# Hybrid encoder layer on one core: the first stage's hand-written order, with places for other work behind every dense product instead of every third, and two product pairs of a scan step placed apart

## The chip, the core and the metric

The program runs on one core of a Trainium2 chip. A core has engines that work side by side: TensorE (PE; weight loads into it are shown as PEld), VectorE (DVE), ScalarE (ACT) and GpSimd (POOL); SyncE (SP) issues most DMAs. Each engine takes its instructions strictly in the order in which they were written into its queue, and waits on semaphores for the others. The metric is the device time of one execution in microseconds (us), lower being better.

## The reference

One layer of an encoder over 16 learned tokens and 1024 positions of width 1024, in float32. A normed input is projected into the inputs of two mixers and two gates; the first mixer is a gated DeltaNet with 8 heads, scanned forwards and backwards:

```python
h = rmsnorm(h_res, norm1_w[l])
proj = h @ w_in[l]
(q, k, v, z, b_raw, a_raw, sc_b, sc_c, sc_x, gate_a, gate_b) = jnp.split(proj, SPLIT_POINTS, axis=-1)
o_dn = gated_deltanet_bidir(q, k, v, z, b_raw, a_raw, dn_conv_w[l], A_log[l], dt_bias[l], dn_norm_w[l])
y_a = o_dn @ w_branch_dn[l]
y_b = (sc_b * depthwise_conv_centred(sc_c * sc_x, sc_conv_w[l])) @ w_branch_sc[l]
merged = jax.nn.sigmoid(gate_a) * y_a + jax.nn.sigmoid(gate_b) * y_b
h_res = h_res + merged @ w_out[l]
...
h_res = h_res + (jax.nn.silu(gu[..., :D_FF]) * gu[..., D_FF:]) @ w_down[l]
```

One chunk of the scan, for each head and direction, carries a state S (128 x 128):

```python
v_new = u_c - jnp.einsum("bhcd,bhde->bhce", w_c, S)
o_c = (jnp.einsum("bhcd,bhde->bhce", qd_c, S)
       + jnp.einsum("bhij,bhje->bhie", qk_c, v_new))
S = S * gl_c[..., None, None] + jnp.einsum("bhcd,bhce->bhde", kd_c, v_new)
```

## The kernel before

**Stages.** The first stage, to about 1061 us, computes all projections of the normed input but the last three z units, and all of the DeltaNet heads; the branches, the output projection and the gated MLP follow. The change lies in the first stage alone.

**Two kinds of work on TensorE.** The dense work is 69 units of 128 output columns each: 24 for q, k, v (three per head), 24 of the short convolution, 16 gates, 5 z. A unit is two or three banks, that is output tiles of 320 to 512 columns in PSUM (the memory in which products accumulate, in banks of 512 float32 columns per partition); a bank takes 24 products (8 pieces of the inner dimension, times high x high, high x low and low x high parts). `dense_steps` (L332) issues them, all from L339. Between them go the *streams*, Python generators that each carry one head through one phase: `g_decay`, `g_norm`, `g_inv` (inverses of the triangular blocks, put together from 32 x 32 pieces) and `g_scan` (the scan). VectorE's long element-wise jobs (convolutions, the substitution of `fs_job`, norms) wait as filler in three lanes.

**The order is written out by hand.** While the program is generated, the clocks `T["pe"]`, `T["dve"]`, `T["act"]` and `T["pool"]` keep planned times; here this bookkeeping is called the planner. `pe(ns)` moves TensorE's clock on and returns it plus HOP (200 ns); `V(n)` and `A(n)` price a VectorE or ScalarE operation of n columns, start it no earlier than TensorE's clock, and return its end plus TOPE (370 ns). A stream issues some instructions and yields the planned time from which its next ones may be issued. Each time a dense unit yields, the main loop (L1328) calls `run_streams` (L967), which resumes every stream whose time has come, and `pump` (L316), which issues filler to VectorE until its clock is 700 ns ahead of TensorE's. Where in each engine's queue an instruction stands is thus settled by the planner; what it waits for is settled by the data, through semaphores.

**Where a unit yields.** `dense_steps` yields behind every third product, having added the price of three. A product of n columns is priced n/2.4 + 13 ns. At four such places (`SPL`, L1323) the split of the next unit's weights into high and low parts is issued in four pieces (L942 and L945): a ScalarE cast, a VectorE subtraction, twice.

**One step of a scan** (L798 to L878) treats two chunks, one forwards (d = 0) and one backwards (d = 1), with two PSUM banks b1 and b2:

1. L805: kT by S into columns 0 and 1 of b1; L808: qT by S into columns 0 and 1 of b2.
2. L815, VectorE: r from b1 and the scaled values vS.
3. L820: NP (the inverse) by r into columns 2 and 3 of b1.
4. ScalarE, from these columns: w twice (L827), then v2 twice (L832; the profile calls it v).
5. L837, the *state products*: kn by w into columns 0 and 1 of b1. L840, the *decayed products*: PQ by v2 into columns 2 and 3 of b2.
6. L849, VectorE: the new S from b1; then the step's output from b2 (L867 to L877).

There are 8 heads of 8 steps; the last step of a head has no state products, so there are 56 pairs of L837 and 64 of L840. A matmul in float32 shows in the profile as two passes, so one pair is a group "x4". The two pairs of point 5 are issued at one place, when w is planned to be ready.

**Inverse and start of a scan.** In `g_inv` four groups of small products (L711, L720 with L723, L741 with L742, L748 with L749) are priced 600, 1050, 1000 and 1000 ns. In `g_scan` the first product (L787) may be issued 1000 ns before the planned time of the last vS (L779).

Of the kernel before, what the change touches and what calls it, by code (L numbers as in the profile page):

```python
# [16 lines left out]
P = 128  # L17
# [30 lines left out]
def encoder_layer(ctx: ExitStack, tc: tile.TileContext, x, meta, norm1_w, w_in, w_ba,  # L48
# [22 lines left out]
    def psm():  # L71
        return ps.tile([P, 512], F32, tag="m", name=uid("pm"), bufs=2)
# [187 lines left out]
    HOP, TOPE, DEP = 200, 370, 127  # L260
    ARRIVE = 10000
    LAND = 5500
    T = {"pe": 0.0, "dve": 0.0, "act": 0.0, "pool": 0.0}

    def on(e, ns, ready=0.0):

        T[e] = max(T[e], ready, T["pe"]) + ns
        return T[e] + TOPE

    def pe(ns):  # L270
        T["pe"] += ns
        return T["pe"] + HOP
# [4 lines left out]
    def A(n):  # L277
        return on("act", 144 + 0.834 * n)
# [49 lines left out]
                lanes[k].pop(0)  # L328

    sweep = ()  # L330

    def dense_steps(po, w, xx, t0, n):  # L332
        (wh, wl), (xh, xl) = w, xx
        t0 += C0
        parts = {"hh": (wh, lambda k: xh[:, k]), "hl": (wh, lambda k: xl[k]), "lh": (wl, lambda k: xh[:, k])}
        seq = [(m, k) for m in sweep for k in range(KT)] if sweep else [(m, k) for k in range(KT) for m in ("hh", "hl", "lh")]
        for i, (m, k) in enumerate(seq):
            ww, f = parts[m]
            mm(po[:, :n], ww[:, k], f(k)[:, t0:t0 + n], start=i == 0, stop=i == 3 * KT - 1)  # L339
            if i % 3 == 2:  # L340
                pe(3 * (n / 2.4 + 13))
                yield

    raws = []
# [6 lines left out]
    def half_buffer():  # L351
        return d1.tile([P, 520], F32, tag="rb", name=uid("rb"), bufs=3)
# [109 lines left out]
    def u_z(h, w):  # L462

        rest = None
        for i in range(2):
            po = psm()
            for k, _ in enumerate(dense_steps(po, w, hx, META + 512 * i, 512)):
                if k == 3 and rest:
                    rest()
                yield  # L470
            th = half_buffer()[:, :512]
            nc.scalar.activation(th, po, AF.Tanh, scale=0.5)
            A(512)

            def rest(i=i, th=th, po=po):
                nc.vector.scalar_tensor_tensor(out=th, in0=th, scalar=1.0, in1=po, op0=ALU.add, op1=ALU.mult)
                V(512)
                nc.sync.dma_start(z_d[h][:, 512 * i:512 * i + 512], th)
        T["dve"] = max(T["dve"], T["act"] + HOP)
        rest()  # L480
# [143 lines left out]
    def g_inv(h, st_):  # L624
# [35 lines left out]
        for j in range(META - 1):  # L660
            n = META - 1 - j
            tm = dn.tile([1, 64], F32, tag="tmm", name=uid("tm"), bufs=1)
            tv = tm[:, :(j + 1) * n].rearrange("p (r i) -> p r i", r=j + 1)
# [45 lines left out]
        for c in range(NC):  # L709
            for d, a, b, Xs, xo in pairs:  # L710
                mm(pt[B(b), c], NP[B(a), c, d, B(b)], Xs[B(a), c, xo:xo + 32], start=True, stop=True)  # L711
        pe(600)
        yield T["pe"] + HOP
        nc.scalar.mul(T2, pt, -1.0)
        yield A(256)
# [2 lines left out]
        for c in range(NC):  # L718
            for d, a, b, Xs, xo in pairs:
                mm(pp[B(a), c], T2[B(b), c], NP[B(b), c, d, B(b)], start=True, stop=True)  # L720
            for d, a, b, Xs, xo in pairs:
                if Xs is X64:
                    mm(px[B(b), c], NP[B(b), c, d, B(b)], T2[B(b), c], start=True, stop=True)  # L723
        pe(1050)
        yield T["pe"] + HOP
        for i, (d, a, b, Xs, xo) in enumerate(pairs):
            if i % 2:
# [12 lines left out]
        for c in range(NC):  # L740
            mm(pt[hi, c], NP[lo, c, 0, hi], X64[lo, c], start=True, stop=True)  # L741
            mm(pt[lo, c], NP[hi, c, 1, lo], X64[hi, c], start=True, stop=True)  # L742
        yield pe(1000)
        nc.scalar.mul(T3, pt, -1.0)
        yield A(512)
        pp = pss().rearrange("p (c i) -> p c i", c=NC)
        for c in range(NC):
            mm(pp[lo, c], T3[hi, c], NP[hi, c, 0, hi], start=True, stop=True)  # L748
            mm(pp[hi, c], T3[lo, c], NP[lo, c, 1, lo], start=True, stop=True)  # L749
        yield pe(1000)  # L750
        nc.scalar.copy(NP[lo, :, 0, hi], pp[lo])
        nc.vector.tensor_copy(NP[hi, :, 1, lo], pp[hi])
        yield max(on("dve", 710), A(512))
# [2 lines left out]
    def g_scan(h, st_):  # L756
# [9 lines left out]
        def newbank():  # L766
            return pss().rearrange("p (a n) -> p a n", a=4)

        for grp in ((8, 0, 7), (1, 2, 3), (4, 5, 6)):
# [7 lines left out]
            for i, c in enumerate(grp):  # L777
                p = META if c == 8 else P
                nc.scalar.activation(vS[:p, c], pt[:p, i], AF.Copy, scale=sk[:p, c:c + 1])  # L779
                A(P)  # L780
        yield T["act"] + HOP - 1000

        oacc = [NP[:, c, c // 4] for c in range(NC)]

# [14 lines left out]
        for i in range(NC):  # L799
            cd = (i, NC - 1 - i)  # L800
            hd = (h, 8 + h)
            act_ = [d for d in range(2) if S[d] is not None]
            b1, b2 = newbank(), newbank()
            for d in act_:
                mm(b1[:, d], kT[:, cs(cd[d])], S[d], start=True, stop=True)  # L805
            t = pe(215 * len(act_))
            for d in act_:
                mm(b2[:, d], qT[:, cs(cd[d])], S[d], start=True, stop=True)  # L808
            pe(215 * len(act_))
            yield t  # L810
            r0 = [vS[:, cd[0]], vS[:, cd[1]]]
            for d in act_:
                c = cd[d]
                r0[d] = dn.tile([P, P], F32, tag=f"r{d}", name=uid("r0"))
                nc.vector.scalar_tensor_tensor(out=r0[d], in0=b1[:, d], scalar=negEG[:, c, hd[d]:hd[d] + 1], in1=vS[:, c],  # L815
                                               op0=ALU.mult, op1=ALU.add)
                t = V(P, 1)
            yield t
            for d in range(2):
                mm(b1[:, 2 + d], NP[:, cd[d], d], r0[d], start=True, stop=True)  # L820
            yield pe(430)
            w = [None, None]
            v2 = [None, None]
            for d in range(2):
                c = cd[d]
                w[d] = dn.tile([P, P], F32, tag=f"w{d}", name=uid("w"))
                nc.scalar.activation(w[d], b1[:, 2 + d], AF.Copy, scale=ce[:, c, d:d + 1])  # L827
                t = A(P)
            for d in range(2):
                c = cd[d]  # L830
                v2[d] = dn.tile([P, P], F32, tag=f"v2{d}", name=uid("v2"))
                nc.scalar.activation(v2[d], b1[:, 2 + d], AF.Copy, scale=cc[:, c, d:d + 1])  # L832
                A(P)
            yield t
            if i < NC - 1:
                for d in range(2):
                    mm(b1[:, d], kn[:, cd[d]], w[d], start=True, stop=True)  # L837
                t = pe(430)
            for d in range(2):
                mm(b2[:, 2 + d], PQ[:, cd[d], d], v2[d], start=True, stop=True)  # L840
            t2 = pe(430)
            if i < NC - 1:
                yield t
                for d in range(2):
                    Sn = dn.tile([P, P], F32, tag=f"S{d}", name=uid("S"), bufs=2)
                    if S[d] is None:
                        nc.vector.tensor_copy(Sn, b1[:, d])
                    else:
                        nc.vector.scalar_tensor_tensor(out=Sn, in0=S[d], scalar=eGl[:, cd[d], hd[d]:hd[d] + 1],  # L849
                                                       in1=b1[:, d], op0=ALU.mult, op1=ALU.add)  # L850
                    t = V(P, 1)
                    S[d] = Sn
            else:
                freed += 1
                yield t2

            for d in range(2):
                c = cd[d]
                eg = eG[:, c, hd[d]:hd[d] + 1]
                first = c not in seen  # L860
                seen.add(c)
                if d not in act_:
                    nc.scalar.copy(oacc[c], b2[:, 2 + d])
                    A(P)
                    continue
                if first:
                    nc.scalar.activation(oacc[c], b2[:, d], AF.Copy, scale=eg)  # L867
                    A(P)
                else:
                    nc.vector.scalar_tensor_tensor(out=oacc[c], in0=b2[:, d], scalar=eg, in1=oacc[c],  # L870
                                                   op0=ALU.mult, op1=ALU.add)
                    V(P, 1)
                nc.vector.tensor_tensor(out=oacc[c], in0=b2[:, 2 + d], in1=oacc[c], op=ALU.add)
                V(P)
                if not first:
                    jk = dn.tile([P, P], F32, tag="jk", name=uid("jk"))
                    nc.scalar.activation(jk, oacc[c], AF.Square, accum_out=sso[:, c:c + 1])  # L877
                    on("act", 310)  # L878
            yield t
# [440 lines left out]
                yield T["act"]  # L1320

    dn = ph1.enter_context(tc.tile_pool(name="dn", bufs=1))
    SPL = (11, 12, 13, 14)  # L1323
    for g in (gen0, gen1):
        for _ in g:
            pass
    decs.append([g_gates(), T["pe"], None])
    while done < H or qkv_units or fill_units or any(ahead):  # L1328
        u = ahead.pop(0)
        if u is None:  # L1330
            run_streams()
            pump()
            T["pe"] += 100
            ahead.append(pick())
            continue
        for k in range(u[3][0], 4):
            split_part(u, k)
        if ahead[0]:
            ahead[0][1] = wtiles([P, KT, P])
        ahead.append(pick())  # L1340
        for n_, _ in enumerate(u[0][1](u[1])):
            if ahead[0] and n_ in SPL:
                split_part(ahead[0], SPL.index(n_))
            run_streams()
            pump()
# [198 lines left out]
    t = KT - 1  # L1544
# [41 lines left out]
    for j in range(NF):  # L1586
# [9 lines left out]
        if j >= HK:  # L1596
            k = j - HK
# [176 lines left out]
```

## Time and profile before

| | |
|---|---|
| median of 3 runs | 2012.12 us (2009.04 to 2012.36) |
| the profiled execution's own time | 2009.61 us |
| its span, first to last instruction | 2007.9 us |
| granted TensorE clock in the span | 0.999 |
| last product of L339 begins | 1060.7 us |
| DVE busy, ACT busy in the span | 1353.8 us, 823.9 us |

How to read the lines that follow. The page gives busy time, its share of the span and the number of instructions of each engine; the row PEclk shows the granted clock in 40 slices of the span, in tenths. A line of stretches begins with the stretch in us and its length, then the busy time (and count) of PE, PEld, DVE, ACT and POOL, the granted clock, the DMA share and GB/s. A line of a group names line, engine, operation, tile names (out<-in) and count, then the shortest, median and longest duration in ns; under it stand the causes of the engine's idle time before such an instruction, with the total in us and the number of times, or those who waited for the group. A row of the timeline gives start, duration (both us), engine, line, operation, tiles, shape, the number of instructions merged in it, and in brackets the engine's idle time before it with what ended it. Matmuls overlap in the array, so a product's duration is longer than the distance to the next start; it is the starts that tell the pace.

### The profile page before, as it was taken

Reading aid. Unit: us, or ns where it says so; the run is one execution under the profiler, and the core shown is the slowest. Engines: PE = TensorE matmul, PEld = TensorE weight load, DVE = VectorE, ACT = ScalarE, POOL = GpSimd, SP = SyncE. Lnnn points to the kernel's source line nnn. Section 1 sums busy time; section 2 is a strip of 40 time slices with the busy share of each in tenths; the row PEclk is TensorE's granted clock in tenths of the full one; section 3 lists DMA queues with packets and bytes.
Section 4 is the critical chain, followed back from the end, with each engine's and each line's share of the span. In section 5 each row is a group of like instructions: output and inputs, shape, how many; then the busy total and the mean of one; then the engine's idle time right before and its main releaser. Section 6 shows DMA issues by size and latency. Waiting matters only on the chain.

```text
span 2007.9 us, 31943 instructions
## 1 busy us (share of the span) xinstructions
PE 1987.4 (99%) x12059; PEld 1727.9 (86%) x12059; DVE 1353.8 (67%) x2966; ACT 823.9 (41%) x1945; POOL 119.6 (6%) x407
## 2 busy tenths in 40 slices
PE   9999999999999999999999999999999999999998
PEld 8999999999999988988888888887888888888887
DVE  6889586888888776866245434468866666646575
ACT  6462345454554464633334211224423333334344
POOL 2002200101020202010000000000000000000000
PEclk9999999999999999999999999999999999999999
DMA  3121222212212232232127633123666345477654
GB/s 138 40 88 64 75 78 71 74 47 76 59 54 85 69 101 64 81 89 94 70 94 247 215 126 116 58 90 109 237 225 221 139 149 186 158 272 244 196 172 167
DMA packets 131409, 247.85 MB, mean 123 GB/s; under 512 B 45045, under 2 KB 54694, under 8 KB 128823
## 3 DMA queue, kind: packets, MB, share of 16 engines
q1 hardware_dynamic: 130679, 244.77, 36.1%
q8 instruction: 94, 1.54, 0.3%
q10 hardware_dynamic: 576, 1.05, 0.1%
q14 instruction: 60, 0.49, 0.1%
HBM read 179.10 MB, written 66.67 MB: 122 GB/s over the span
## 4 chain that ended last, share of the span: by engine, by line
PE 90%; DVE 5%; ACT 2%; DMA 1%; issue 1%; SPq 0%; ACTq 0%; DVEq 0%
PE pm L339 36%; PE pd L1514 10%; PE pe L1514 4%; PE pm L1514 3%; PE pe L589 1%; PE pd L820 1%; PE pe L134 1%; PE pe L135 1%; PE pe L133 1%; PE pd L840 1%; PE pd L134 1%; PE pd L133 1%; PE pd L135 1%; PE pe L1682 1%; PE pe L1680 1%; PE pd L837 1%
## 5 line engine op out<-in xcount | busy, mean ns | idle before, releaser
L339 PE MATMUL pm<-hTh,wh 128*128 128x512 f32 (+4 forms) x1424 | 518.2, 369 | 0.8 <-ACT kq L391 0.5
L339 PE MATMUL pm<-hTh,wl 128*128 128x512 f32 (+4 forms) x1424 | 483.4, 344 | 0.0
L339 PE MATMUL pm<-al,wh 128*128 128x512 f32 (+4 forms) x1424 | 482.6, 343 | 0.0
L339 PEld LDWEIGHTS pm<-hTh,wh 128*128 128x128 f32 x1424 | 267.0, 188 | 20.4 <-issue 1.7
L339 PEld LDWEIGHTS pm<-hTh,wl 128*128 128x128 f32 x1424 | 266.1, 188 | 19.8 <-DVE wl L942 0.3
L339 PEld LDWEIGHTS pm<-al,wh 128*128 128x128 f32 x1424 | 267.4, 189 | 14.5
L101 DVE TENSOR_TENSOR al<-raw,ring_h 128x1024 fp32r<-128x1024 f32 x73 | 88.8, 1224 | 65.4 <-ACT ring_h L100 64.6
L942 DVE TENSOR_TENSOR wl<-raw,wh 128x512 fp32r<-128x512 f32 x134 | 91.0, 690 | 51.0 <-ACT wh L945 50.5
L100 ACT CAST ring_h<-raw 128x1024 fp32r<-128x1024 f32 x73 | 76.8, 1055 | 106.8 <-PE pd L1682 35.5
L361 DVE SCALAR_TENSOR_TENSOR kq<-ra,wc,kq 128x520 f32<-128x520 f32 x128 | 96.9, 757 | 3.3 <-ACT kq L391 1.7
L945 ACT CAST wh<-raw 128x512 fp32r<-128x512 f32 x134 | 79.2, 622 | 13.3 <-PE pm L339 9.6
L100 ACT CAST wh<-raw 128x1024 fp32r<-128x1024 f32 x43 | 45.2, 1052 | 85.8 <-PE pe L134 35.2
L827 ACT ACTIVATE w<-pd,small 128x128 f32<-128x128 f32 x128 | 40.2, 366 | 84.8 <-PE pd L820 79.7
L498 DVE TENSOR_TENSOR fP<-fP,tm 128x135 f32<-128x135 f32 (+23 forms) x248 | 71.3, 288 | 4.9
L494 DVE TENSOR_TENSOR tm<-fP,fN 128x135 f32<-128x135 f32 (+23 forms) x248 | 71.2, 287 | 4.4
L849 DVE SCALAR_TENSOR_TENSOR S<-S,eGl,pd 128x128 f32<-128x128 f32 x104 | 31.9, 345 | 52.0 <-PE pd L837 33.9
L1516 DVE TENSOR_TENSOR b<-pd,b 128x512 f32<-128x512 f32 x22 | 15.2, 691 | 68.5 <-PE pd L1514 68.5
L1617 ACT ACTIVATE b<-b 128x512 f32<-128x512 f32 x22 | 13.9, 633 | 114.8 <-DVE b L1516 114.8
L101 DVE TENSOR_TENSOR wl<-raw,wh 128x1024 fp32r<-128x1024 f32 x43 | 52.4, 1220 | 12.3 <-ACT wh L100 12.2
L664 POOL TENSOR_TENSOR tm<-mP,mN 1x15 f32<-1x15 f32 (+7 forms) x120 | 42.9, 358 | 218.7 <-DMA mN<-ndm 210.2
L1514 PE MATMUL pd<-b_hl,wh 128*128 128x512 f32 x176 | 54.4, 390 | 0.0
L361 DVE SCALAR_TENSOR_TENSOR vT<-ra,wc,vT 128x520 f32<-128x520 f32 x64 | 48.4, 756 | 3.6 <-ACT vT L391 2.6
(523 smaller groups left out, 4416.9 us busy)
## 6 DMA issues: line engine op xcount, KB each, us to landing
raw<-in_w_in_dram SPq DMA_DIRECT2D x72, 512.0 KB
raw<-in_w_gate_up_dram SPq DMA_DIRECT2D x44, 512.0 KB
sums<-in_w_down_dram SPq DMA_DIRECT2D x22, 512.0 KB
t_d<-sums SPq DMA_DIRECT2D x11, 1024.0 KB
raw<-s_d SPq DMA_DIRECT2D x44, 256.0 KB
raw<-t_d SPq DMA_DIRECT2D x44, 256.0 KB
act_d<-b SPq DMA_DIRECT2D x43, 256.0 KB
raw<-act_d SPq DMA_DIRECT2D x33, 256.0 KB
```

Source lines behind the costliest of these rows:

```text
L100: nc.scalar.copy(hi, src)
L101: nc.vector.tensor_tensor(out=lo, in0=src, in1=hi.bitcast(F32), op=ALU.subtract)
L133: mm(po[:m, :n], wh[:, k, :m], xhk[:, t0:t0 + n], start=(k == 0), stop=False)
L339: mm(po[:, :n], ww[:, k], f(k)[:, t0:t0 + n], start=i == 0, stop=i == 3 * KT - 1)
L361: nc.vector.scalar_tensor_tensor(out=acc, in0=raw[:, h0 + t:h0 + t + hn], scalar=wc[:, t, col:col + 1], in1=acc, op0=ALU.mult, op1=ALU.add)
L494: nc.vector.tensor_tensor(out=tv, in0=fP[:, 0:r, j:j + 1].broadcast_to([P, r, n]), in1=fN[:, j:j + 1, j + 1:32].broadcast_to([P, r, n]), o ...
L498: nc.vector.tensor_tensor(out=fP[:, 0:r, j + 1:32], in0=fP[:, 0:r, j + 1:32], in1=tv, op=ALU.subtract)
L664: nc.gpsimd.tensor_tensor(out=tv, in0=mP[:, 0:j + 1, j:j + 1].broadcast_to([1, j + 1, n]), in1=mN[:, j:j + 1, j + 1:META].broadcast_to([1, ...
L827: nc.scalar.activation(w[d], b1[:, 2 + d], AF.Copy, scale=ce[:, c, d:d + 1])
L942: nc.vector.tensor_tensor(out=u[1][1][:, k], in0=u[2][:, k], in1=u[1][0][:, k].bitcast(F32), op=ALU.subtract)
L945: nc.scalar.copy(u[1][0][:, k], u[2][:, k])
L1514: mm(po, x[:, k], y, start=k + i == 0 and not add_to, stop=k == 3 and i == 2, skip_group_check=add_to)
```

## The change

`dense_steps` prices every product by itself and, once the streams run, yields behind each of them (`fine`). The positions that counted yields are rewritten: the four weight splits from yields 11, 12, 13, 14 to 33, 36, 39, 42, and the z units' postponed operation from yield 3 to 11. In a scan step, a second wait is put between the state products and the decayed products: the former are issued when w is planned ready, the latter when v2 is. The state's new S (L849) is issued, as before, behind both. The planner's prices of the inverse's groups become 870, 1140, 1270 and 1270 ns, and the scan's first product waits for the planned time of the last vS plus HOP.

```diff
     sweep = ()
+    fine = {"on": False}
...
             mm(po[:, :n], ww[:, k], f(k)[:, t0:t0 + n], start=i == 0, stop=i == 3 * KT - 1)
-            if i % 3 == 2:
-                pe(3 * (n / 2.4 + 13))
+            pe(n / 2.4 + 13)
+            if fine["on"] or i % 3 == 2:
                 yield
...
-                if k == 3 and rest:
+                if k == 11 and rest:
                     rest()
...
-        pe(600)
+        pe(870)
...
-        pe(1050)
+        pe(1140)
...
-        yield pe(1000)
+        yield pe(1270)
         nc.scalar.mul(T3, pt, -1.0)
...
-        yield pe(1000)
+        yield pe(1270)
         nc.scalar.copy(NP[lo, :, 0, hi], pp[lo])
...
-        yield T["act"] + HOP - 1000
+        yield T["act"] + HOP
...
                 nc.scalar.activation(v2[d], b1[:, 2 + d], AF.Copy, scale=cc[:, c, d:d + 1])
-                A(P)
-            yield t
+                tv = A(P)
             if i < NC - 1:
+                yield t
                 for d in range(2):
                     mm(b1[:, d], kn[:, cd[d]], w[d], start=True, stop=True)
                 t = pe(430)
+            yield tv
             for d in range(2):
                 mm(b2[:, 2 + d], PQ[:, cd[d], d], v2[d], start=True, stop=True)
             t2 = pe(430)
...
-    SPL = (11, 12, 13, 14)
+    SPL = (33, 36, 39, 42)
...
     decs.append([g_gates(), T["pe"], None])
+    fine["on"] = True
     while done < H or qkv_units or fill_units or any(ahead):
```

## The prediction

> **What bounds the kernel now.** I read the page first, then busy time by stretches, then the groups of the lines that the diff touches with what their engine waited for, and last the timeline of single steps.
>
> ```profile
> span 2007.9 us, 31943 instructions
> PE 1987.4 (99%) x12059; PEld 1727.9 (86%) x12059; DVE 1353.8 (67%) x2966; ACT 823.9 (41%) x1945; POOL 119.6 (6%) x407
> PEclk9999999999999999999999999999999999999999
> ```
> ```profile
> 445.00:499.00 54.00, 54.00 (x360) 50.85 (x359) 45.62 (x134) 23.79 (x74) 9.25 (x36) 1.00 0.19 57
> 974.00:1032.00 58.00, 58.00 (x329) 49.94 (x329) 21.54 (x61) 21.25 (x65) 0.00 (x0) 1.00 0.19 69
> 1032.00:1061.00 29.00, 29.00 (x134) 24.01 (x133) 11.52 (x34) 7.96 (x17) 0.00 (x0) 1.00 0.36 118
> ```
>
> TensorE (third column of the stretches) is full: in the scans of the third and of the last head, and in the 29 us behind the last scan, in which only dense products are left. Its clock is full throughout. So the first stage lasts as long as TensorE's own work plus what TensorE stands still. An earlier scan gains nothing, because dense products follow it until 1061 us. The change keeps every product; it can move the end only through standstill, and that must be looked for in places where the overlapped rows hide it from the busy share.
>
> ```profile
> L837 PEld LDWEIGHTS pd<-w,kn x224: 186/190/192, 237.8 to 1023.9; 128*128 128x128 f32 x112
> ...
>   ACT v L832: 2.4, 11
> ```
> ```profile
> L820 PEld LDWEIGHTS pd<-r,NP x240: 186/189/192, 235.3 to 1028.7; 128*128 128x128 f32 x120
> ...
>   DVE r L815: 9.7, 16
> ```
> ```profile
>   PEld pd L820: 6.2, 10
>   PE pd L820: 3.4, 6
> ```
>
> The state products (L837) waited 11 times, 2.4 us in all, and not for w, which they read, but for **v**, which only the decayed products (L840) read. The products with NP (L820) waited for r; the last fence (who waited for L815) shows that the 9.7 us count one standstill twice, at the weight load and at the product, so I use the 6.2 us of the weight loads. About 8.6 us is thus all that better placing of a scan's products can win.
>
> **Why L837 waits for v.** One step beside dense products of 322 columns, and one beside 512, without the rows of weight loads and other engines' work (start, duration):
>
> ```profile
> 249.74 0.61 PE L820 MATMUL pd<-r,NP 128*128 128x128 f32 x4
> 250.10 0.39 PE L339 MATMUL pm<-hTh,wh 128*128 128x322 f32 x1
> 250.43 0.63 ACT L827 ACTIVATE w<-pd,small 128x128 f32<-128x128 f32 x2 [2.57 <-PE pd L820]
> 250.95 0.63 ACT L832 ACTIVATE v<-pd,small 128x128 f32<-128x128 f32 x2
> ...
> 251.37 0.31 PE L339 MATMUL pm<-hTh,wl 128*128 128x322 f32 x1
> 251.63 0.71 PE L837 MATMUL pd<-w,kn 128*128 128x128 f32 x4
> 252.18 0.61 PE L840 MATMUL pd<-v,PQ 128*128 128x128 f32 x4
> ```
> ```profile
> 887.56 0.38 PE L820 MATMUL pd<-r,NP 128*128 128x128 f32 x2
> 887.92 0.47 PE L339 MATMUL pm<-hTh,wh 128*128 128x512 f32 x1
> 888.23 0.39 PE L339 MATMUL pm<-al,wh 128*128 128x512 f32 x1
> 888.46 0.39 PE L339 MATMUL pm<-hTh,wl 128*128 128x512 f32 x1
> 888.72 0.63 ACT L832 ACTIVATE v<-pd,small 128x128 f32<-128x128 f32 x2
> ...
> 889.16 0.40 PE L339 MATMUL pm<-hTh,wl 128*128 128x512 f32 x1
> ...
> 889.85 0.40 PE L339 MATMUL pm<-hTh,wl 128*128 128x512 f32 x1
> 890.08 0.61 PE L837 MATMUL pd<-w,kn 128*128 128x128 f32 x4
> 890.53 0.61 PE L840 MATMUL pd<-v,PQ 128*128 128x128 f32 x4
> 890.89 0.48 PE L339 MATMUL pm<-hTh,wh 128*128 128x512 f32 x1
> 891.21 0.40 PE L339 MATMUL pm<-al,wh 128*128 128x512 f32 x1
> ```
>
> At 322, w was whole at 250.43 + 0.63 = 251.06, v at 251.58, and L837 began at 251.63, 0.05 behind v, although the turn of the last dense product before it (251.37) would have let it go at 251.52. In the code, both come from the bank b1: L837 writes its columns 0 and 1 while ScalarE's w and v read its columns 2 and 3, so the write must wait for the last read. The wait is in the data's places, and the changed kernel keeps them: both v activations are still issued ahead of L837.
>
> The Trainium skill, page "PSUM — Partial Sum Buffer", section "PSUM bank collisions raise a hardware error", says that a TensorE write and a ScalarE read in one bank and the same partitions at once are an error whichever columns they touch, and that software is to guard by bank. By that rule the second rival below has no chance, and the trace agrees with the 0.05 us; the sum does not use it.
>
> **The change, part by part.**
>
> *L837's place.* The planner prices a 128-column ScalarE operation at 144 + 0.834 x 128 = 251 ns and calls w ready 2 x 251 + 370 = 872 ns after the place where it is issued, which is the first one at least 200 ns behind L820's products. Before, places lie three dense products apart. At 512 that is 3 x 226 = 679 ns: w at the first place, L837 two places on, nine dense products behind L820 (in the second fence the first, 887.92, to the last, 889.85). By then v had long been whole; at 512 L837 began 890.08 - 889.35 = 0.73 us behind v. That rounding was the cover. Now a place lies behind each product. At 512: w issued behind one, L837 behind 1 + 4 = 5 (4 x 226 = 905 >= 872). L837's turn comes where the sixth dense row stands, at 889.16, that is 1.60 us behind L820's start. It can go only at v's end, 888.72 + 0.63 = 889.35, plus 0.05: 889.40. So 0.24 us late. A late product also shows its weight load: L837's four passes take 0.71 where late and 0.61 where not. Price **0.34 us**. At 322 or 320 (147 ns): w behind two, L837 behind 2 + 6 = 8, where the ninth row stands (251.37); it goes at 251.63: 0.26 + 0.10 = **0.36**. At 336 (153 ns), also eight: 8 x 6 ns later, so 0.26 - 0.05 + 0.10, about 0.3. At 384 (173 ns), eight: 8 x 26 = 0.21 later than at 320, 0.05 late or not at all; I take 0.06 for half the weight load.
>
> Going through the 56 places in the timeline, 41 of them have the regular nine products between: 20 beside 512, 8 beside 384, 5 beside 336, 6 beside 320 or 322, 2 mixed. Price 20 x 0.34 + 8 x 0.06 + 5 x 0.3 + 8 x 0.35 = 6.8 + 0.5 + 1.5 + 2.8 = 11.6 us. In the other 15, L837 came three or more products later, because the planner holds ScalarE for busy; there it may stay clear. Unknown between 0 and 15 x 0.36 = 5.4; I take 2.2, nearer the low end, as most of these rows were clear of v by more than one place. The 2.4 us of today goes in return. Sum **+11.4** (9.2 to 14.6). Behind a late L837 on TensorE stands everything else, in order, so nothing covers it.
>
> *L840 apart.* Its ready time is 4 x 251 + 370 = 1374 ns behind w's issue; L837's place plus the planner's 430 ns is at least 872 + 430 = 1302. So at most one dense product comes between. Price of the split: a four-pass group costs 887.92 - 887.56 = 0.36 plus its dense follower's surplus, 0.31 - 0.23 = 0.08; the eight-pass group costs 890.89 - 890.08 = 0.81, and 0.32 - 0.23 = 0.09. Two small make 0.88, one large 0.90: nothing, within 0.02 x 56 = 1 us either way. The state's update (L849) is now issued behind L840, about half a microsecond later on VectorE; its reader, L805, never waits in the trace, and a late scan costs nothing before 1061 us.
>
> *L820's place.* The planner prices a 128-column VectorE operation at 130 + 1.042 x 128 = 263 ns and calls r ready 2 x 263 + 370 = 896 ns behind its issue. In steps of three (679, 519, 459, 439 ns) that was 1358, 1038, 918 or 1317 ns (512, 384, 336, 320); in single ones it is 905, 1038, 918, 1024. L820 loses 0 to 0.45 us of cover, 0.25 in the mean. Where it is late today, VectorE was held by something else:
>
> ```profile
> 280.15 0.61 ACT L945 CAST wh<-raw 128x512 fp32r<-128x512 f32 x1
> 280.79 0.69 DVE L942 TENSOR_TENSOR wl<-raw,wh 128x512 fp32r<-128x512 f32 x1 [1.04 <-ACT wh L945]
> 281.40 0.60 DVE L815 SCALAR_TENSOR_TENSOR r<-pd,negEG,vS 128x128 f32<-128x128 f32 x2
> 282.06 0.71 PE L820 MATMUL pd<-r,NP 128*128 128x128 f32 x4 [0.75 <-DVE r L815]
> ```
>
> The low part of the next unit's weights waited in VectorE's queue for its cast, and r behind it. The diff moves these splits by at most two dense products, so such meetings go on. Ten late ones with up to 0.25 us less cover make +2.5; some fall away by chance: I take **+1.5**, between -6.2 (all gone) and +7 (twice as many).
>
> *The rest* I take as **0**: the planner's prices for the inverse's four product groups go up, so what follows them is issued later and safer; the first product of a scan is placed up to 1 us later; the z units' leftover operation stays behind the twelfth product. The streams' DMAs keep their order among themselves; on SP's queue they only come up to two products earlier, and POOL's work as well. Bounds 1 us either way.
>
> **Sum.** 11.4 + 1.5 = +12.9 us. On the profiled execution's 2009.61 us that is 2022.5; the median shown, 2012.12, lies 2.5 above it, which would make 2025.0. I say **2024**. Own range: 2016 to 2032.
>
> **Rivals.**
> 1. *VectorE becomes the bound of the step.* Finer places also let the filler be handed out more often, so its queue is fuller when r is issued. If a third of the 64 L820 groups come late at today's 0.6 us (6.2 / 10), that is 13 - 6.2 = +7: 2012.1 + 11.4 + 7 = 2030. For it: VectorE busy 45.6 of 54 us in the third head's scan. Against: 21.5 of 58 in the last. Chance 0.10.
> 2. *L837 goes with w (not slower).* If the wait could end with w, at 251.06 and not 251.58, it would be met in every place above (the earliest turn, 251.37, is later). The 2.4 us goes, 1.5 comes: about 2011. It decides as soon as L837 rows begin before v's end. Against: the 0.05 us. Chance 0.10.
> 3. *Faster.* The order on VectorE falls out so that r is never behind a waiting split, and ScalarE's turn is planned so late that v is whole too: -8.6, about 2003.5. For it: 15 of 56 places are planned late already. Against: the 41 others. Chance 0.11.
> 4. *The split does nothing*, since L840 follows L837 at once. Likely so, and it changes no term; the forecast hangs on L837's place.
>
> **How the numbers follow.** The forecast has 0.69, rival 1 0.10: slower 0.79. No change, within 0.2% (4 us, about what a measurement of this kernel can tell), has rival 2's 0.10; faster 0.11. The range 2008 to 2032 takes in rival 2 and leaves out rival 3 and the upper tail.
>
> **What would show it.** In the changed profile L837's row should name v with some 12 to 16 us in 35 to 50 waits, and beside 512 each scan step should show five dense rows between L820 and L837, with L837 0.05 us behind v and 0.71 us long. L820's waits for r should stay at 5 to 10 us, and the last scan should end earlier before the last dense product. Wrong it would be if L837 began before v's end, if its waits stayed at 2 us, or if the stage of L339 ended within 4 us of 1061.

## The result and the profile after

The changed kernel takes 2031.31 us (median of 5 runs, 2030.08 to 2032.84) against 2009.40 us before: a ratio of 1.0106, 95% interval 1.0091 to 1.0121. It is slower, by about 22 us or 1.1%. The profiled execution took 2032.53 us with a span of 2030.8. In the changed file the lines of the scan stand one to two further down: L805 is L806, r is L816, NP by r L821, w L828, v L833, the state products L838, the decayed products L842, the new S L851, the dense products L340.

The page of the changed kernel, span, engines and TensorE's clock:

```profile
span 2030.8 us, 31965 instructions
PE 2001.7 (99%) x12059; PEld 1726.3 (85%) x12059; DVE 1349.6 (66%) x2966; ACT 821.3 (40%) x1945; POOL 122.8 (6%) x407
PEclk9999999999999999999999999999999999999999
```

The same 12059 products, the same clock, and VectorE and ScalarE are busy 4 and 3 us less. The time is TensorE's standstill. PE's busy share, 99% before and after, doesn't show it, as the rows overlap; the starts of the products do. The groups of dense products and of decayed products tell where (duration shortest/median/longest, first and last start):

```profile
L340 PE MATMUL pm<-hTh,wl x1424: 302/334/586, 17.7 to 1082.1; 128*128 128x512 f32 x58, 128*128 128x320 f32 x40, 128*128 128x384 f32 x40, 128*128 128x336 f32 x24
L842 PE MATMUL pd<-v,PQ x256: 270/275/275, 230.3 to 967.0; 128*128 128x128 f32 x128
```

The last dense product begins at 1082.1 in place of 1060.7: 21.4 of the 22.9 us of span were lost in the first stage. The scans themselves end earlier, at 967.0 and not 1031.3, and it is worth nothing: 115 us of dense products follow in place of 29. Who waited for whom, TensorE's weight loads, longest in total first (us, times, longest):

```profile
PEld pd L838 <- ACT v L833: 17.5, 45, 0.6
PEld pd L821 <- DVE r L816: 8.0, 18, 1.0
PEld pe L590 <- PE pm L340: 3.9, 5, 1.1
PEld pd L742 <- issue: 3.5, 8, 1.1
...
PEld pd L793 <- DVE w L791: 2.9, 5, 1.0
```

Before, the first row had 2.2 us in 10 waits and the second 6.2 in 10; L589 (now L590) had 0.3 us in one, and L792 (now L793) waited for VectorE 0.8 us in three places, never for w. The third row names a dense product as what ended the weight load's wait; the product L590 itself waited for VectorE:

```profile
PE pe L590 <- DVE PQ L617: 2.1, 4, 0.8
```

One step of the last head beside 512 columns, with TensorE's products and v alone:

```profile
934.54 0.71 PE L821 MATMUL pd<-r,NP 128*128 128x128 f32 x4 [0.19 <-DVE r L816]
935.00 0.49 PE L340 MATMUL pm<-hTh,wl 128*128 128x512 f32 x1
935.33 0.39 PE L340 MATMUL pm<-hTh,wh 128*128 128x512 f32 x1
935.56 0.39 PE L340 MATMUL pm<-al,wh 128*128 128x512 f32 x1
935.79 0.40 PE L340 MATMUL pm<-hTh,wl 128*128 128x512 f32 x1
935.85 0.62 ACT L833 ACTIVATE v<-pd,small 128x128 f32<-128x128 f32 x2
936.02 0.40 PE L340 MATMUL pm<-hTh,wh 128*128 128x512 f32 x1
936.53 0.71 PE L838 MATMUL pd<-w,kn 128*128 128x128 f32 x4
937.00 0.48 PE L340 MATMUL pm<-al,wh 128*128 128x512 f32 x1
937.32 0.49 PE L842 MATMUL pd<-v,PQ 128*128 128x128 f32 x3
```

Five dense products stand between L821 and L838, not nine. The fifth began at 936.02, so the next product's turn was at 936.25; L838 began at 936.53, 0.06 behind v's end (935.85 + 0.62 = 936.47), and took 0.71 us in place of 0.61. One dense product lies between the two pairs, as in 39 of the 56 steps; in the others there is none.

To size this without the overlap of weight loads I took, for each of the 56 steps, the time from the start of the dense product before the two pairs to that of the second dense product behind them, less those dense products at their own pace. The mean is 1158 ns, before 949 ns: 56 x 0.209 = **11.7 us**. The same measure for the 64 L821 groups gives 560 against 543 ns, 1.1 us. That leaves 21.4 - 12.8 = **8.6 us** for the other streams' products; among the rows that grew are those of L590, L793, the transposes at L97, L742 with L743, L749 and L806.

Two of these, traced, are late behind VectorE. First a pair of L590, then an L793, with VectorE's rows before each:

```profile
507.24 0.20 DVE L600 TENSOR_TENSOR small<-beta,small 128x18 f32<-128x18 f32 x1
507.54 0.22 DVE L601 TENSOR_SCALAR Nm<-Nm,small 16x16 f32<-16x16 f32 x1
507.69 0.60 DVE L613 SCALAR_TENSOR_TENSOR NP<-pe,small,PQ 128x128 f32<-128x128 f32 x2
508.32 0.42 DVE L617 TENSOR_TENSOR PQ<-pe,PQ 128x256 f32<-128x256 f32 x1
508.89 0.67 PE L590 MATMUL pe<-kq 128*128 128x256 f32 x2 [0.83 <-DVE PQ L617]
```
```profile
738.84 0.42 DVE L641 STREAM_TRANSPOSE NP<-NP 32x256 f32<-32x256 f32 x1
739.20 0.12 DVE L510 TENSOR_TENSOR small<-small 128x9 f32<-128x9 f32 x1
739.34 0.43 DVE L641 STREAM_TRANSPOSE NP<-NP 32x256 f32<-32x256 f32 x1
739.80 0.34 DVE L791 TENSOR_SCALAR w<-pd,small 16x128 f32<-16x128 f32 x1
740.20 0.48 PE L793 MATMUL pd<-w,kn 16*128 16x128 f32 x2 [0.72 <-DVE w L791]
```

L590 needs a bank that L617 reads, and L617 came behind a row of small operations of its own stream. In the code both are issued at one place, 200 ns before VectorE's planned time, so that little but the rounding of places stood between them. L793 needs w of L791, and two transposes of the next head's inverse (L641) stood before it: the plan had VectorE free earlier than it was.

### The profile page after: what moved, and what is told of

The parts are those of the page before. It is cut to its first block, busy times and chain, and to the rows that moved or that the text cites. A ratio compares the mean times of both kernels' runs of the same rounds, so it can differ in the third digit from the quotient of the medians.

```text
span 2030.8 us, 31965 instructions
## 1 busy us (share of the span) xinstructions
PE 2001.7 (99%) x12059; PEld 1726.3 (85%) x12059; DVE 1349.6 (66%) x2966; ACT 821.3 (40%) x1945; POOL 122.8 (6%) x407
## 4 chain that ended last, share of the span: by engine, by line
PE 49%; DVE 2%; DMA 1%; ACT 1%; issue 0%; SPq 0%; DVEq 0%; ACTq 0%
PE pd L1517 10%; PE pm L340 6%; PE pe L1517 4%; PE pm L1517 3%; PE pe L135 1%; PE pe L133 1%; PE pe L134 1%; PE pd L135 1%; PE pd L133 1%; PE pd L134 1%; PE pe L1685 1%; PE pe L1684 1%; PE pe L1683 1%; PE pd L1685 1%; PE pd L1684 1%; PE pd L1683 1%
## 5 line engine op out<-in xcount | busy, mean ns | idle before, releaser
L340 PE MATMUL pm<-hTh,wl 128*128 128x512 f32 (+4 forms) x1424 | 495.9, 353 | 0.7 <-DVE wl L944 0.7
L340 PE MATMUL pm<-hTh,wh 128*128 128x512 f32 (+4 forms) x1424 | 495.7, 353 | 0.8 <-ACT ra L433 0.4
L340 PE MATMUL pm<-al,wh 128*128 128x512 f32 (+4 forms) x1424 | 495.5, 353 | 0.0
L340 PEld LDWEIGHTS pm<-hTh,wh 128*128 128x128 f32 x1424 | 266.8, 188 | 19.9 <-issue 1.1
L340 PEld LDWEIGHTS pm<-hTh,wl 128*128 128x128 f32 x1424 | 267.1, 188 | 19.0 <-DVE wl L944 1.9
L340 PEld LDWEIGHTS pm<-al,wh 128*128 128x128 f32 x1424 | 267.0, 188 | 16.9
L828 ACT ACTIVATE w<-pd,small 128x128 f32<-128x128 f32 x128 | 40.1, 365 | 82.0 <-PE pd L821 67.0
L851 DVE SCALAR_TENSOR_TENSOR S<-S,eGl,pd 128x128 f32<-128x128 f32 x104 | 31.6, 342 | 36.1 <-PE pd L838 18.1
L533 ACT ACTIVATE PQ<-PQ,negG 128x128 f32<-128x128 f32 x128 | 43.0, 394 | 17.8 <-DVE PQ L528 17.8
```

Source lines behind the costliest of these rows:

```text
L533: nc.scalar.activation(PQ[:, c, d], PQ[:, c, d], AF.Exp, bias=negG2[:, c, hd:hd + 1])
```

## The experiments

Each was timed in rounds with the kernel before, which had 2009.7 to 2010.3 us; the ratio is to that.

Below, the *fine grid* has a place behind each dense product, the *grid of three* one behind every third, and *cover* is the time between the moment when a product's inputs are ready and its turn.

**1. State products at v, on the fine grid.**

```diff
             if i < NC - 1:
-                yield t
+                yield tv
                 for d in range(2):
                     mm(b1[:, d], kn[:, cd[d]], w[d], start=True, stop=True)
```

> The changed kernel with one line different: the state products (L838) are issued when v is planned ready, not w, so both pairs stand together again, on the fine grid. Theory (the state products meet v in the bank): L838's waits fall from 18.0 us to under 2, the mean cost of a step's two pairs from 1158 ns to about 905, 56 x 0.253 = 14 us, so about 2017 us, and about 8 us above the kernel before stay, which must come from elsewhere (L590, L793, L821, L742). Rival (VectorE's fuller queue makes everything late, L838's wait only shows it): above 2028.

2022.92 us, ratio 1.0063 (1.0049 to 1.0077). No row names v any more, and the two pairs cost 900 ns in the mean, so (1158 - 900) x 56 = 14.4 us of standstill are gone, as the theory says. But only 8.4 us came back. Its waits by weight load:

```profile
PEld pd L821 <- DVE r L816: 11.6, 22, 1.0
PEld pe L590 <- PE pm L340: 4.2, 7, 0.9
...
PEld pd L806 <- DVE S L851: 2.9, 6, 1.1
```

The products that need r and S wait 3.6 and 2.3 us longer, which makes up the difference: it seems that VectorE had been catching up while TensorE stood at L838. 13 us above before remain, where 8 had been expected.

**2. v not read from the bank.**

```diff
-                nc.scalar.activation(v2[d], b1[:, 2 + d], AF.Copy, scale=cc[:, c, d:d + 1])
+                nc.scalar.activation(v2[d], w[d], AF.Copy, scale=cc[:, c, d:d + 1])
```

> The changed kernel, but the v activations (L833) read w's tile in SBUF and not the PSUM bank b1; v's values differ from the reference's. Nothing else moves. Theory (the wait is for ScalarE's reads of the bank that L838 writes): L838 begins before v's end, its waits go, and the time is within 2 us of the kernel with the state products at v, about 2017. Rival (L838 waits for v for another reason, or TensorE is late anyway): L838 still 0.05 us behind v's end and 2031.

2023.90 us, ratio 1.0065 (1.0053 to 1.0078): within 1 us of the first run, as expected, though both lie 6 to 7 us above the 2017 expected. One step of it, again beside 512:

```profile
934.64 0.61 PE L821 MATMUL pd<-r,NP 128*128 128x128 f32 x4
935.00 0.48 PE L340 MATMUL pm<-al,wh 128*128 128x512 f32 x1
935.32 0.39 PE L340 MATMUL pm<-hTh,wl 128*128 128x512 f32 x1
935.33 0.63 ACT L828 ACTIVATE w<-pd,small 128x128 f32<-128x128 f32 x2 [1.66 <-PE pd L821]
935.55 0.39 PE L340 MATMUL pm<-hTh,wh 128*128 128x512 f32 x1
935.78 0.39 PE L340 MATMUL pm<-al,wh 128*128 128x512 f32 x1
935.85 0.69 ACT L833 ACTIVATE v<-w,small 128x128 f32<-128x128 f32 x2
936.00 0.40 PE L340 MATMUL pm<-hTh,wl 128*128 128x512 f32 x1
936.24 0.61 PE L838 MATMUL pd<-w,kn 128*128 128x128 f32 x4
```

L838 is placed as in the changed kernel, behind five dense products, and goes at its turn, 0.30 us **before** v's end (936.54). So the wait hung on v's reads of the bank that L838 writes. The two pairs cost about 900 ns here too, with one dense product between them in 39 of the 56 steps. This run, too, left r late (12.0 us in 26 waits).

**3. Only the split, on the grid of three.**

```diff
-                A(P)
-            yield t
+                tv = A(P)
             if i < NC - 1:
+                yield t
...
+            yield tv
             for d in range(2):
                 mm(b2[:, 2 + d], PQ[:, cd[d], d], v2[d], start=True, stop=True)
```

> The kernel before with only the second wait of the scan step added: state products when w is planned ready, decayed products when v is, on the grid of three products. Theory (the rounding to three products covers v; a split as such costs nothing): L837's wait stays near 2.4 us, the time within 2 us of before, 2008 to 2012. Rival (two small groups cost more than one large one): 64 x 0.1 us or more, 2016 and up.

2010.89 us, ratio 1.0005 (0.9996 to 1.0013); L837's weight loads wait 2.3 us in 11. On the old grid the early place costs nothing, nor does the split; but here the coarse places set only 17 of the 56 pairs apart, so that run 2 is the better test of the split.

**4. Both pairs at v, on the grid of three.** In the kernel before, the planned time of the second v (`t = A(P)`) takes the place of w's.

> The kernel before with both pairs issued when v is planned ready, on the grid of three. Theory: the 2.4 to 2.7 us of L837's waits go and nothing else comes, 2006 to 2008 us. Rival (a scan a place later costs at its end, or the wait moves to the next product): 2009.4 or more.

2008.62 us, ratio 0.9993 (0.9984 to 1.0002). L837's waits are gone, as expected, but the time is 0.6 us above the range expected, and the gain can't be told from none.

**5 and 6. The fine grid in halves.** From here on the question was the 13 us that the first run left. `dense_steps` notes whether a product is the third; in run 5 only the filler, in run 6 only the streams wait for that.

```diff
+            fine["third"] = i % 3 == 2
             if fine["on"] or i % 3 == 2:
                 yield
...
             run_streams()
-            pump()
+            if fine["third"]:
+                pump()
```

> The kernel with the state products at v on the fine grid, and VectorE's filler handed out only behind every third product, as before; the streams still at every product. Theory A (lost cover: ready times that hang on VectorE are planned too early, and rounding to three products hid it): little changes, 2019 to 2024 us, waits for r (L821) 8 us or more. Theory B (filler handed out three times as often stands in VectorE's queue ahead of the streams' work): waits for r fall to 6 us or less, 2010 to 2015.

> The other half: the state products at v, streams resumed only behind every third product, filler handed out behind each. Theory A: the cover is back, waits for r 3 to 6 us, L590's and L806's gone, 2007 to 2012 us. Theory B: the filler still stands in the way, 2016 to 2023.

2021.00 us, ratio 1.0057 (1.0043 to 1.0071), and 2018.96 us, 1.0046 (1.0033 to 1.0058). Theory A met its range in run 5 and missed it in run 6; theory B the other way round. Neither half is the cause alone.

**7. Cover given back.** On the fine grid with the state products at v, each ready time that a VectorE operation returns is 450 ns later:

```diff
-        return T[e] + TOPE
+        return T[e] + TOPE + (450 if e == "dve" else 0)
```

> The fine grid with the state products at v, and every planned ready time that comes from a VectorE operation 450 ns later, the most cover that the change took (at 512 columns). Theory A: the late groups of L821, L590, L793, L742 and L806 go, 2008 to 2013 us. Rival (VectorE is overloaded and only gets later by the same amount): 2020 or more.

2008.09 us, ratio 0.9991 (0.9982 to 1.0000). The 13 us are gone: L821's weight loads wait 4.1 us and L590's waits are no longer among the longest. VectorE was not overloaded; much of what hung on it was planned too early. L590's own place goes by VectorE's clock and not by such a ready time, so the 450 ns don't move it directly; by what way its waits went isn't shown.

```profile
PEld pd L821 <- DVE r L816: 4.1, 8, 0.9
...
PEld pm L340 <- ACT kq L392: 1.2, 3, 0.7
PEld pd L721 <- ACT T L715: 1.2, 1, 1.2
```

**8. Cover for r on the grid of three**, with both pairs at v: `t = V(P, 1) + 450` before L820.

> The grid of three, both pairs at v, and the products that need r (L820) planned 450 ns later. Theory A: on the coarse grid too the 5 to 6 us of waits for r are a planning error that cover removes, while scans that end later cost nothing as long as dense products last: 2002 to 2006 us. Rival (scans then outlast the dense products): above 2010.

2007.08 us, ratio 0.9984 (0.9976 to 0.9993): faster than both kernels, though 1 us short of the range expected. L820's waits fall to 1.9 us in 4; the last scan now ends with the last dense product, at 1055 us, so there is no more to give away in this order.

**9. Both halves in thirds**, with the changed kernel's prices and split places, state products at v.

> The changed kernel's prices, split places and postponed first product, state products at v, but streams and filler both taken up only behind every third product. Each half alone stayed 9 to 11 us above before. Theory AB (streams at every product and filler at every product each use up the cover): with both in thirds 2007 to 2011 us. Theory C (the prices, the first product's place or the split places cost it, common to both halves): 2016 or more.

2015.70 us, ratio 1.0032 (1.0020 to 1.0044): between the two theories. The rounding is back whole, and with it about 6 of the 13 us (1.0063 to 1.0032). In this file L822 is NP by r and L591 the product of L590:

```profile
PEld pd L822 <- DVE r L817: 5.3, 9, 1.2
...
PEld pe L591 <- PE pm L340: 0.4, 1, 0.4
```

These two are about where they were before the change (6.2 and 0.3 us), so their waits did come from the lost rounding. What holds the rest is in other rows.

**10. The old prices on the fine grid**, with the old early first product, state products at v.

> The fine grid with the state products at v, with the old prices of the inverse's groups and the old early first product of a scan. Theory AB: 2020 to 2025 us, as with the new ones. Theory C: 2010 to 2015.

2029.86 us, ratio 1.0098 (1.0084 to 1.0112): above the ranges of both theories. Beside run 1 (1.0063) the new prices and the later first product together gain some 7 us on the fine grid; they are no cause of the loss.

**11. The new prices on the grid of three**, state products at v, split places as before.

> The kernel before with both pairs at v, the new prices and the first product at the vS's planned time; split places as before. Theory AB: 2007 to 2010 us. Theory C, if the prices or the first product's place are the cause: 2015 or more; if it is the split places: as under AB, while the run with both in thirds is late.

2006.75 us, ratio 0.9986 (0.9977 to 0.9994), faster than both kernels like run 8, and just under the range of theory AB. With run 9 this follows theory C's second branch: the two runs differ in the split places (in units of two banks of 512 and in the convolution's, two dense products earlier) and hardly in anything else, and lie 9 us apart. In run 9 no one row holds them: the weight loads of L822 (r) wait 2.5 us longer, those of the dense products, L713 and L722 1 to 2 us each. Runs 1, 9 and 11 thus take the loss apart: some 6 us with the grid, 9 with the split places. Whether the places as such cost that, or any other order of the same instructions would scatter as much, stays open; no run moves the splits alone on the fine grid.

**12. Twice the cover on the fine grid.**

> The fine grid, state products at v, ready times from VectorE 900 ns later in place of 450. With 450 the last scan ended 69 us before the last dense product, so there is time to give away. Theory AB: the 4 us of waits for r go, 2003 to 2007 us. Rival (what is left are VectorE's long waits, which no cover of this size meets): 2007 to 2010.

2013.37 us, ratio 1.0018 (1.0009 to 1.0027): above the ranges of theory and rival, and worse than with 450. Its waits show v again, in 6 places, though L838 is planned for v, and r more often than with 450:

```profile
PEld pd L821 <- DVE r L816: 5.8, 10, 1.0
...
PEld pd L838 <- ACT v L833: 2.6, 6, 0.6
...
PEld pd L97 <- DVE NP L891: 1.8, 7, 0.3
```

## Why the prediction was right, and where it fell short

*TensorE's standstill sets the end.* Right: the same products at the same clock, 21.4 us more standstill in the first stage, and scans that end 64 us earlier without any gain.

*L837's place.* Right in mechanism and in size. The wait is for v, because v is read from the bank that L837 writes (run 2 takes that away and the wait goes); five dense products beside 512, 0.05 to 0.06 behind v, 0.71 us long. +11.4 was forecast, +11.7 measured. The row of waits came out higher than the 12 to 16 us that were to show it, 17.5 at the weight loads, since a weight load's idle time begins while the product before it still runs. 45 of the 56 places waited, within the 35 to 50 forecast.

*L840 apart.* Right: 0 forecast; run 2's pairs, set apart in 39 of 56 steps, cost no more than run 1's that stand together, and run 3 shows 1.0005 (0.9996 to 1.0013).

*L820's place.* +1.5 forecast, 1.1 measured in the changed kernel; but this number was held down by L838's standstill. Without it r's waits rise by 3.6 us (run 1).

*The rest, 0 within 1 us.* This is the step that failed: 8.6 us. I had given the loss of cover only to the products that wait for r, though L590, L793, L742 and L806 hang on VectorE's planned times in the same way and lost the same rounding. That none of them waited much before was no proof of slack, only of the grid. For r and L590 run 9 shows this: with the rounding back their waits are back too. But it returns only about 6 of run 1's 13 us; the other part goes with the split places, which the prediction saw moved "by at most two dense products" and gave no price of their own; there the cause stays open. That 450 ns of cover on VectorE's times take the whole loss away (run 7) shows a remedy, not that lost cover was all of it. Nor were the new prices without effect: with the later first product they gain about 7 us on the fine grid (runs 1 and 10), where 0 had been put.

*The sum.* 2024 forecast, 2031.3 measured, inside the range and near its top. On the times before, 2012.1 and 2009.4, that is a rise of 11.9 forecast and 21.9 measured, so half of the loss was foreseen. That the time lies in the range is luck in this respect: its room was meant for L837 and r, and what filled it was the term that was to be 0 within 1 us. Rival 1 named the right engine, in more places than r, but not the reason: with the filler handed out as seldom as before, r's waits stay at 12.2 us and the time at 2021 (run 5). Rivals 2 and 3 fell with L838's waits and the time. Rival 4 was right in its own matter: at most one dense product between the pairs, no price.

What stays open is why each half of the fine grid alone still costs 9 to 11 us (runs 5 and 6) and what makes run 9 slower than run 11. That both use up cover agrees with run 7, but runs 9 and 12 show that small changes of the order move the time by some microseconds in a way that I can't derive.

## What to carry to other kernels

Where an order is written by hand on a coarse grid, the rounding is cover that nobody has written down: before making the grid finer, look for every wait that the plan does not know (here a bank that one engine reads while another is to write it) and give each planned time the cover that it had. Place a product when all that its queue entry really waits for is ready, not only its operands; the profile's row of who waited for whom names that, even where it shows only 2 us. And on a full engine an earlier side stream is worth nothing: here the best two kernels, 0.9984 (0.9976 to 0.9993) and 0.9986 (0.9977 to 0.9994), kept the old grid; one gave r more time, the other had the new prices. Run 7, on the fine grid, can't be told from them (0.9991, 0.9982 to 1.0000), and all three gains are smaller than what a change of order alone may move.

## What the runs showed of the hardware

A product that comes late costs more than its lateness: L838's four passes take 0.71 us where it waited and 0.61 where it did not, in 0.10 us of weight load that is otherwise under way during the product before. And a small change of the instructions' order moved this kernel by several microseconds, with the same work on every engine: 2008.1 us with 450 ns of cover, 2013.4 with 900.
